# Gated-linear-attention level products cut to 64 by 64 on both halves of the array, gathered into one run a head

## The chip, the cores and the metric

The kernel runs on one core of one Trainium2 chip. Times are device microseconds of one execution. The kernel before took 2210.24 us as the median of 3 runs (2208.63 to 2212.44). Its profile is one further execution.

The engines are called as in the profile: PE is the matrix engine (PEld its weight loads), DVE the vector engine, ACT the scalar engine, POOL the general engine, SP the engine that issues most DMAs. A line number such as L873 is a line of the kernel before.

## What is computed

One layer of a hybrid decoder over 2048 tokens and 16 leading meta tokens, width 1024, everything in float32:

```
u      = RMSNorm(h);  proj = u @ w_in                 # one combined projection
y_ssd  = SSD branch   (16 heads of 64, 4 groups, state 128, chunk 128)
y_gla  = GLA branch   (4 heads, key width 128, value width 256)
out    = RMSNorm(h + (sum_b sigmoid(g_b) * (y_b @ w_branch[b])) @ w_out)
```

The change lies in the gated linear attention (GLA). For one head and one chunk of tokens it needs, for every pair t >= s,

```
gc   = cumsum(log_a)                                  # per key channel k
att[t, s] = sum_k q[t,k] * k[s,k] * exp(gc[t,k] - gc[s,k])
o    = att @ v  +  (q * exp(gc)) @ state
```

The factor exp(gc[t] - gc[s]) can't be split into one factor of t and one of s without overflow over a whole chunk, so the kernel works in levels, described below.

## The kernel before, in words

**Stages.** The 2048 tokens go in four blocks of 512. In the first part of the kernel (to about 1445 us of the profile) each block is projected and both branches are computed; in the second part come the merge gates, the branch products and the output product. The change touches the first part only.

**Levels.** `gla_scan` handles one head of one block: 512 tokens as four chunks of 128 (`NCH`). For each half in `LEVELS` = 64, 32, 16, 8, 4, 2, `level_in` (L845) takes the gates relative to the middle of every group of 2*half tokens (a DVE subtraction, L858), exponentiates both sides on ACT (L861, L862), and multiplies the first half of each group with the keys (L863) and the second half with the queries (two instructions of L865) into one tile `kq`. Chunks lie in pairs in it: the query half of one chunk takes the place that the key half of its neighbour leaves free, so that one 128 by 128 product serves two chunks. `level_out` (L869) then makes two such products a level (L873), each float32 product being two PE instructions, and puts the result into a tile `xa` of 128 by 2 by 128: with a copy on ACT for level 64 (L877), under a mask on DVE (`copy_predicated`, L880) for the others. Of a level below 64 only the 64 by 64 blocks on the diagonal are used, of level 64 only the two off it. The pairs at distance one and the diagonal come from sums over the key channel with a matrix of ones (L945); they are merged at L947 to L953 into `att`, which holds all four chunks. `split` turns `att` into a rounded part and a rest (`atp`), the odd chunks after a transposition (L960).

**Ticks.** `enter` walks through the pieces of projection of a block: a piece is some 24 products of 512 columns. After each piece `step` runs every begun generator up to its next `yield`; that is a tick. So PE sees: a piece, then what each scan has in this tick, then the next piece. A GLA scan begins every sixth piece. In a scan of the kernel before, the first tick has `level_in(64)`; the second `turn_keys` (a transposition of the keys, L894), levels 32 and 16 in and level 64 out; the third 8 and 4 in, 32 and 16 out; the fourth 2 in, 8 and 4 out, and the operands `pn`, `pd` of the sums; the fifth level 2 out, the sums and the merge; the sixth the transpositions and the first half of `advance`; the seventh and eighth the outputs (L981 and the products after it); the tenth the transposition of the output (L1000, drained by L1001 on DVE).

**Where scans meet.** In blocks 1 and 2 (counting from 0) the heads begin behind pieces 30, 36, 42 and 48 (the last is the first piece of the next block), so the fourth tick of one head is the tenth of the head before it. Piece 36 to 39 is `proj_v12`, which holds three banks of PSUM pool `pj` and one of `pt`. In the last block heads 2 and 3 begin inside `proj_v12` and `proj_v`, behind pieces 39 and 43, and there `step` goes through the scans from the youngest to the oldest.

**What sets the order.** The order on PE and SP is the one in which the program is written (`manual_schedule`). The order on DVE, ACT and POOL is chosen beforehand by a planner that simulates the program; `issue_after(x)` puts what a block of code issues on x's engine behind x. Each engine then runs its queue in that order and waits for its operands and for free buffers.

**Buffers.** SBUF tiles of one tag share `bufs` slots. Tag `sq` (2 KB a partition, 6 slots) serves `ex` and `kq` of the levels, `pd` and its split, `att`, and in `ssd_scan` the masked scores `scm` and four decay tiles `dm` a group. Tag `xd` (1 KB, 4 slots) holds `xdt` of `ssd_scan`; tag `c1` (1 KB, 8 slots) serves `xa`, `pn` and its split, the states, `xw` and `yo`. PSUM has three banks each in `pj` and `pt` and two in `pc`; a level's products lie in `pc`, as do the outputs of `advance`, L981 and the inner product of `ssd_scan`. That inner product (`inside`, L717) is already cut in two: 64 columns of weights, 64 moving columns, written to partitions 0 to 63 and 64 to 127 in turn, 32 products (64 instructions) in one run.

Of the kernel before, what the change touches and what calls it, by code (L numbers as in the profile page):

```python
# [8 lines left out]
F32 = mybir.dt.float32  # L9
# [3 lines left out]
AF = mybir.ActivationFunctionType  # L13
ALU = mybir.AluOpType

P = 128
# [3 lines left out]
BLK = 512  # L20
NCH = BLK // P
# [2 lines left out]
NH = 16  # L24
EPS = 1e-6
NWR = 3
NSQ = 6
NT4 = 5
NACT = 8
NC1 = 8  # L30
NAS = 6
LATE_G = 2
LEVELS = (64, 32, 16, 8, 4, 2)
# [10 lines left out]
def trunk_kernel(ctx: ExitStack, tc: tile.TileContext, xm, xmt, w_feat, w_tok, w_v3, w_zm, w_br, w_o,  # L44
                 cf32, cmsk, pvec, fnw, hvec, gw2, out):
    nc = tc.nc
# [5 lines left out]
    def mk(pool, shape, dt, tag, **kw):  # L52
        cnt[0] += 1
        return pool.tile(shape, dt, tag=tag, name=f"{tag}_{cnt[0]}", **kw)
# [72 lines left out]
    bpool, wk, sm, const = pool1("bpool", 1), pool1("wk", 2), pool1("sm", 4), pool1("const", 1)  # L127
# [4 lines left out]
    pc = ctx.enter_context(tc.tile_pool(name="pc", bufs=2, space=bass.MemoryType.PSUM))  # L132
# [4 lines left out]
    def bank(pool, tag):  # L137
        return mk(pool, [P, 512], F32, tag)
# [5 lines left out]
    tris = cst[:, 2:4, :]  # L144
# [126 lines left out]
    def split(h, lo, src):  # L271
        nc.scalar.activation(h, src, AF.Copy)
        nc.vector.tensor_tensor(lo, src, h.bitcast(F32), op=ALU.subtract)
# [117 lines left out]
    msk = const.tile([P, NMSK, P], U8, name="msk")  # L391
# [86 lines left out]
    def gates(o):  # L478
        m0, tt, chunks, g_all = o.m0, o.tt, o.chunks, o.g_all
        ast = (act_tile(F32R) if m0 else mk(wk, [P, BLK], F32R, "sq", bufs=NSQ))[:48, :tt]  # L480
        for a, n in ([(0, META), (m0, BLK)] if m0 else [(0, BLK)]):
# [135 lines left out]
            feats.append(f)  # L617
            yield

    cbs, evicted, convd = {}, [], []  # L620

    def behind():
        return tc.issue_after(evicted[-1].ins) if evicted else nullcontext()
# [6 lines left out]
    def ssd_scan(o, g):  # L630
# [7 lines left out]
        def hb(t, n):  # L638
            return t.unsqueeze(2).to_broadcast([n, 4, 64])

        if m0:
            ps = bank(pt, "pt")
# [20 lines left out]
                                tri.unsqueeze(1).to_broadcast([P, NCH, P]), op=ALU.mult)  # L663
        yt = mk(wk, [P, NCH, 256], F32, "tok4", bufs=NT4)
        ssq = mk(sm, [P, 4], F32, "ssq")
        held, intra = {}, {}

        def before(c):
            a = m0 + c * P
            ci = ci0 + c  # L670
            if c + 1 < NCH:
                fetch_cb(o, g, c + 1)
            cb = cbs.pop((g, c))
            ps = bank(pt, "pt")
            for j, f in enumerate((x0, x1, bf)):
                nc.tensor.transpose(ps[:, j * P:(j + 1) * P], f[:, a:a + P], ident)
            px = ps[:, :256].rearrange("p (h c) -> p h c", c=64)
            xdt = mk(wk, [P, 4, 64], F32, "xd", bufs=NCH)
            nc.vector.tensor_tensor(xdt, px, hb(tkd[:, ci, hs], P), op=ALU.mult)
            xw = mk(wk, [P, 4, 64], F32, "c1", bufs=NC1)  # L680
            nc.vector.tensor_tensor(xw, px, hb(wde[:, ci, hs], P), op=ALU.mult)
            nc.vector.tensor_tensor(yt[:, c].rearrange("p (h c) -> p h c", c=64), px,
                                    hb(d_skip[:, hs], P), op=ALU.mult)
            bt = mk(wk, [P, P], F32, "bt")
            nc.scalar.activation(bt, ps[:, 256:384], AF.Copy)
            dm = mk(wk, [P, 4, P], F32, "sq", bufs=NSQ)
            with behind() if o.b == 0 else nullcontext():
                for h in range(4):
                    nc.scalar.activation(dm[:, h], cb[:, h], AF.Relu, scale=-1.0,
                                         bias=tkc[:, ci, 4 * g + h:4 * g + h + 1])  # L690
                nc.scalar.activation(dm, dm, AF.Exp, scale=-1.0)
            convd[:] = [nc.vector.tensor_tensor(dm, dm, scm[:, c].unsqueeze(1).to_broadcast([P, 4, P]), op=ALU.mult)]
            held[c], intra[c] = (xw, bt), (xdt, dm)
# [53 lines left out]
        r = rstd_of(ssq, 4, 1.0 / 1024)  # L747
# [5 lines left out]
        for j in range(2):  # L753
            ps = bank(pt, "pt")
# [56 lines left out]
    def gla_scan(o, h, last=False):  # L811
# [27 lines left out]

        xa = mk(wk, [P, 2, P], F32, "c1", bufs=NC1)
        kqs = {}

        def level_in(half):  # L845
            nb = BLK // (2 * half)
            npc = P // (2 * half)

            def view(t):
                return t.rearrange("p (b two h) -> p b two h", two=2, h=half)  # L850

            def view5(t):
                return t.rearrange("p (r o b two h) -> p r o b two h", o=2, b=npc, two=2, h=half)

            ex = mk(wk, [P, BLK], F32, "sq", bufs=NSQ)
            kq = mk(wk, [P, BLK], F32, "sq", bufs=NSQ)
            ev = view(ex)
            nc.vector.tensor_tensor(  # L858
                ex.rearrange("p (b s) -> p b s", s=2 * half), gr.rearrange("p (b s) -> p b s", s=2 * half),
                view(gr)[:, :, 0, half - 1:half].to_broadcast([P, nb, 2 * half]), op=ALU.subtract)  # L860
            nc.scalar.activation(ev[:, :, 0], ev[:, :, 0], AF.Exp, scale=-ITEMP)  # L861
            nc.scalar.activation(ev[:, :, 1], ev[:, :, 1], AF.Exp, scale=ITEMP)  # L862
            nc.vector.tensor_tensor(view(kq)[:, :, 0], ev[:, :, 0], view(k)[:, :, 0], op=ALU.mult)  # L863
            for i in range(2):
                nc.vector.tensor_tensor(view5(kq)[:, :, 1 - i, :, 1], view5(ex)[:, :, i, :, 1],  # L865
                                        view5(q)[:, :, i, :, 1], op=ALU.mult)
            kqs[half] = kq

        def level_out(half):  # L869
            kq = kqs.pop(half)  # L870
            ps = bank(pc, "pc")
            for r in range(2):
                nc.tensor.matmul(ps[:, r * P:(r + 1) * P], kq[:, 2 * r * P:(2 * r + 1) * P],  # L873
                                 kq[:, (2 * r + 1) * P:(2 * r + 2) * P], start=True, stop=True)
            pv2 = ps[:, :256].rearrange("p (r t) -> p r t", t=P)
            if half == 64:
                nc.scalar.activation(xa, pv2, AF.Copy)  # L877
            else:
                mi = msk[:, LEVELS.index(half)].unsqueeze(1).to_broadcast([P, 2, P])
                nc.vector.copy_predicated(xa, mi, pv2)  # L880

        level_in(64)
        yield
        if m0:
            ps = bank(pt, "pt")
# [5 lines left out]
        def turn_keys():  # L891
            ps = bank(pt, "pt")
            for c in range(NCH):
                nc.tensor.transpose(ps[:, c * P:(c + 1) * P], kd[:, m0 + c * P:m0 + (c + 1) * P], ident)  # L894
            kdt.extend(beside_64("kdt") for _ in range(2))
            split(*[t.rearrange("p c t -> p (c t)") for t in kdt], ps)

        if not last:
            turn_keys()
        level_in(32)  # L900
        level_out(64)
        level_in(16)
        yield
        if m0:
            ps = bank(pt, "pt")
            nc.tensor.matmul(ps[:, :256], btm[:META], s_gla[:META, h], start=True, stop=True)
            nc.vector.tensor_copy(s_gla[:, h], ps[:, :256])
        level_out(32)
        level_in(8)
        level_out(16)  # L910
        level_in(4)
        yield
        level_out(8)
        level_in(2)
        level_out(4)


        def halves(t):
# [1 line left out]

        pn = mk(wk, [P, 2, P // 2, 2], F32, "c1", bufs=NC1)
        for i in range(2):
# [12 lines left out]
            split(*hl, src)  # L935
            parts.append((hl, n))
        yield
        if last:
            turn_keys()
        level_out(2)  # L940
        sums_ = []
        for hl, n in parts:
            ps = bank(pt, "pt")
            for i in range(2):
                nc.tensor.matmul(ps[:, :n], ones_r, hl[i], start=i == 0, stop=i == 1)  # L945
            sums_.append(ps)
        nc.vector.copy_predicated(xa, msk[:, len(LEVELS)].unsqueeze(1).to_broadcast([P, 2, P]),  # L947
                                  sums_[0][:, :256].rearrange("p (r t) -> p r t", t=P))
        att = mk(wk, [P, NCH, P], F32, "sq", bufs=NSQ)
        nc.vector.tensor_tensor(att.rearrange("p (r o) t -> p r o t", o=2),  # L950
                                xa.unsqueeze(2).to_broadcast([P, 2, 2, P]),
                                tris.unsqueeze(1).to_broadcast([P, 2, 2, P]), op=ALU.mult)
        nc.vector.copy_predicated(att, msk[:, 0].unsqueeze(1).to_broadcast([P, NCH, P]),  # L953
                                  sums_[1].rearrange("p (c t) -> p c t", t=P))
        atp = [beside_64("atp") for _ in range(2)]
        split(*[t[:, 0::2] for t in atp], att[:, 0::2])
        yield
        ps = bank(pt, "pt")
        for r in range(2):
# [30 lines left out]
        with tc.issue_after(summed[-1].ins) if o.b == nblk - 1 and h == GH - 1 and summed else nullcontext():  # L990
            r = rstd_of(ssq, 4, 1.0 / 256)
# [5 lines left out]
        for j in range(2):  # L997
            ps = bank(pt, "pt")
# [68 lines left out]
    for b in range(nblk):  # L1067
        o = new_block(b, next_u[b])
        last = b == nblk - 1
# [331 lines left out]
    for si, st in enumerate(stages):  # L1401
        for q in range(0 if si else 12, 28):
            p, j = PS[q // 4], q % 4
# [12 lines left out]
    for key, st in zip(late, (stages[0], stages[-4])):  # L1416
        i, end = begins[stages.index(st)] + 9, begins[stages.index(st) + 1] - 16
# [88 lines left out]
def _layout(inputs):  # L1506
# [36 lines left out]
    row, col = idx[:, None], idx[None, :]  # L1543
    cf32[:, 2] = col > row
    cf32[:, 3] = col < row
    cmsk = np.zeros((P, NMSK, P), f)
    cmsk[:, 0] = np.eye(P)
    for i, h in enumerate(LEVELS + (1,)):
        if i:
            cmsk[:, i] = (row // (2 * h) == col // (2 * h)) & (row // h != col // h)  # L1550

    def pcol(v):
        return v.reshape(-1, P).T
# [37 lines left out]
```

## Time and profile before

| | |
|---|---|
| median of 3 runs | 2210.24 us (2208.63 to 2212.44) |
| the profiled execution | 2209.51 us, of which the profile's span is 2207.7 us |
| first part, to 1445 us | PE busy 1419.2 of 1445 us |
| second part | PE busy 755.3 of 762 us |
| level products (L873) | 384 instructions, 24 a head and block, 16 of these |
| granted PE clock | 0.997 in the mean |

How to read it: busy time of PE counts a matrix product from its start to its modelled end, and neighbours overlap. What a product takes out of PE's time is therefore the step from one start to the next, not its duration. "Idle before" names what ended a wait of the engine just before an instruction. A wait of an engine that isn't the bound costs nothing by itself.

### The profile page before, as it was taken

How to read it: one execution, taken by the hardware profiler on the slowest of the kernel's cores; microseconds unless marked ns; L12 is line 12 of the kernel's file. 1: busy time of each engine (PE TensorE's matmuls, PEld its weight loads, DVE VectorE, ACT ScalarE, POOL GpSimd, SP SyncE). 2: the span in 40 equal slices, each digit the busy share in tenths (PEclk: the TensorE clock that was granted, in tenths of full speed). 3: DMA queues.
4: the chain of work that ended last, by engine and by line, in shares of the span. 5: the costliest groups of instructions: out<-in, count | busy, mean ns of one | idle time of the engine just before them, and what ended most of it. 6: DMA issues, size and time to landing. Idle time of an engine off the chain costs nothing.

```text
span 2207.7 us, 35845 instructions
## 1 busy us (share of the span) xinstructions
PE 2174.5 (98%) x12301; PEld 1867.9 (85%) x12301; DVE 1553.8 (70%) x2871; ACT 1188.5 (54%) x2767; POOL 693.8 (31%) x689
## 2 busy tenths in 40 slices
PE   7999999999999999999999999999999999999998
PEld 7999889888888988888988888878888888888887
DVE  5786675677577676658677666674789955789876
ACT  5666655466455456545465554464644545554544
POOL 5444433222222122221222100166233374324341
PEclk9999999999999999999999999999999999999999
DMA  9766775667778677778677664376768866787753
GB/s 316 254 228 235 255 271 211 218 217 244 257 253 265 210 227 230 249 257 274 208 223 238 215 216 161 124 265 214 246 221 297 304 223 216 240 286 255 255 187 121
DMA packets 313702, 518.00 MB, mean 235 GB/s; under 512 B 28080, under 2 KB 162480, under 8 KB 313520
## 3 DMA queue, kind: packets, MB, share of 16 engines
q1 hardware_dynamic: 247008, 419.89, 58.3%
q10 hardware_dynamic: 65872, 93.74, 11.6%
q8 instruction: 96, 1.57, 0.3%
q0 software_dynamic: 640, 2.10, 0.2%
q14 instruction: 86, 0.70, 0.1%
HBM read 368.42 MB, written 147.19 MB: 234 GB/s over the span
## 4 chain that ended last, share of the span: by engine, by line
PE 86%; DVE 4%; ACT 3%; DMA 3%; POOL 1%; issue 1%; SPq 1%; POOLq 0%; ACTq 0%; DVEq 0%
PE pj L223 19%; PE pj L225 19%; PE pj L224 19%; PE pt L225 4%; PE pt L224 4%; PE pt L223 4%; PE pc L223 2%; PE pc L224 2%; PE pc L225 2%; PE pc L873 2%; PE pc L717 1%; PE pc L701 1%; PE pc L981 1%; PE pc L700 1%; DVE acc L612 1%
## 5 line engine op out<-in xcount | busy, mean ns | idle before, releaser
L223 PE MATMUL pj<-ue,whl 128*128 128x512 f32 (+2 forms) x672 | 236.7, 352 | 2.3 <-ACT acc L608 2.2
L224 PE MATMUL pj<-ue,whl 128*128 128x512 f32 (+2 forms) x672 | 228.9, 341 | 0.0
L225 PE MATMUL pj<-ue,whl 128*128 128x512 f32 (+2 forms) x672 | 228.5, 340 | 0.0
L223 PE MATMUL pj<-uo,whl 128*128 128x512 f32 x512 | 206.0, 402 | 0.0
L225 PE MATMUL pj<-uo,whl 128*128 128x512 f32 x512 | 199.9, 390 | 0.0
L224 PE MATMUL pj<-uo,whl 128*128 128x512 f32 x512 | 199.5, 390 | 0.0
L223 PE MATMUL pj<-b,a 128*128 128x512 f32 (+1 forms) x484 | 187.4, 387 | 0.5 <-DVE io L1304 0.5
L224 PE MATMUL pj<-b,a 128*128 128x512 f32 (+1 forms) x484 | 187.4, 387 | 0.0
L225 PE MATMUL pj<-b,a 128*128 128x512 f32 (+1 forms) x484 | 187.4, 387 | 0.0
L612 DVE SCALAR_TENSOR_TENSOR acc<-cin,hcw,acc 128x512 f32<-128x512 f32 (+1 forms) x192 | 156.1, 813 | 29.2 <-ACT acc L608 27.5
L1157 POOL TENSOR_TENSOR as<-ar,ar 128x512 f32<-128x512 f32 x38 | 58.3, 1534 | 371.4 <-DMA ar<-in_w_br 124.7
L83 POOL TENSOR_TENSOR wr<-wr 128x256 f32<-128x256 f32 x80 | 69.7, 871 | 332.2 <-DMA wr<-y 142.0
L1186 DVE TENSOR_TENSOR a<-ar,a 128x512 fp32r<-128x512 f32 x160 | 132.1, 834 | 58.8 <-ACT a L1185 57.8
L223 PEld LDWEIGHTS pj<-ue,whl 128*128 128x128 f32 x672 | 127.2, 189 | 18.3 <-ACT acc L608 3.1
L186 POOL TENSOR_TENSOR whl<-wr,whl 128x512 fp32r<-128x512 f32 (+1 forms) x76 | 102.6, 1357 | 122.0 <-ACT whl L184 93.4
L225 PEld LDWEIGHTS pj<-ue,whl 128*128 128x128 f32 x672 | 127.1, 189 | 14.4
L224 PEld LDWEIGHTS pj<-ue,whl 128*128 128x128 f32 x672 | 127.7, 190 | 13.3
L1186 DVE TENSOR_TENSOR a<-as,a 128x512 fp32r<-128x512 f32 x120 | 104.8, 875 | 41.5 <-ACT a L1185 38.2
L1185 ACT ACTIVATE a<-ar 128x512 fp32r<-128x512 f32 x160 | 99.1, 626 | 58.6 <-PE pt L225 22.1
L1220 ACT ACTIVATE sn<-pj 128x512 f32<-128x512 f32 x118 | 70.2, 595 | 110.8 <-PE pj L225 71.0
L224 PE MATMUL pt<-b,a 128*128 128x512 f32 x320 | 124.5, 389 | 0.0
L225 PE MATMUL pt<-b,a 128*128 128x512 f32 x320 | 124.5, 389 | 0.0
(335 smaller groups left out, 6367.9 us busy)
## 6 DMA issues: line engine op xcount, KB each, us to landing
whl<-k_s SPq DMA_DIRECT2D x96, 512.0 KB, 4.1
whl<-k_g SPq DMA_DIRECT2D x96, 512.0 KB, 4.5
whl<-k_v SPq DMA_DIRECT2D x36, 512.0 KB, 3.8
wr<-in_w_feat SPq DMA_DIRECT2D x64, 256.0 KB, 4.1
k_s<-whl SPq DMA_DIRECT2D x32, 512.0 KB, 3.8
cb<-cumd SPq DMA_DIRECT2D x64, 256.0 KB, 4.7
y<-gg ACTq DMA_DIRECT2D x64, 256.0 KB, 4.2
k_g<-whl SPq DMA_DIRECT2D x32, 512.0 KB, 3.7
```

Of the source, the lines that this page charges most:

```text
L83: nc.gpsimd.tensor_tensor(o, x, y, op=ALU.subtract)
L186: nc.gpsimd.tensor_tensor(hl[:, 1], raw, hl[:, 0].bitcast(F32), op=ALU.subtract)
L223: nc.tensor.matmul(ps, sh, mh, start=first, stop=False, **kw)
L224: nc.tensor.matmul(ps, sh, ml, start=False, stop=False, **kw)
L225: nc.tensor.matmul(ps, sl, mh, start=False, stop=last, **kw)
L612: convd[:] = [nc.vector.scalar_tensor_tensor(acc, cin[:, k:k + tt], hcw[:, ti, k:k + 1], acc, op0=ALU.mult, op1=ALU.add)]
L700: nc.tensor.matmul(ps[:, :256], cf[:, a:a + P], s_ssd[:, g], start=True, stop=True)
L873: nc.tensor.matmul(ps[:, r * P:(r + 1) * P], kq[:, 2 * r * P:(2 * r + 1) * P], kq[:, (2 * r + 1) * P:(2 * r + 2) * P], start=True, stop=True)
L1157: nc.gpsimd.tensor_tensor(s1, a21, a22, op=ALU.add)
L1185: nc.scalar.activation(t[:, 0], src, AF.Copy)
L1186: latest[:] = [nc.vector.tensor_tensor(t[:, 1], src, t[:, 0].bitcast(F32), op=ALU.subtract)]
L1220: nc.scalar.activation(sn, self.ps[n, "a"], AF.Copy)
```

## The change

Six edits:

1. Each level product of 128 by 128 is replaced by two of 64 by 64, one on each half of the array's columns (`levels_out`): 4 products a level and 24 a head, for 12 before.
2. All six levels of a head are multiplied in one run, in the fourth tick, into two `pc` banks taken together: levels 64, 32, 16, 8 in the first, 4 and 2 in the second. The merge moves from the fifth tick to the fourth; the fifth then has only `turn_keys` of the very last head.
3. Operands come two levels a tick: 64 and 32, then 16 and 8, then 4 and 2 with `pn` and `pd`.
4. `xa` shrinks to 128 by 2 by 64. Level 64 is copied straight into `att` by two ACT instructions of 64 partitions, the places opposite are zeroed by two POOL memsets, level 32 is copied by ACT, and 16, 8, 4, 2 follow under the mask on DVE, 128 elements a partition. The pairs at distance one and the product with the triangle are done in two instructions of 64 partitions each. The masks are built for this layout.
5. The subtraction of the next head's level 64 is put behind the last instruction of the merge (`merged`).
6. Buffers: `sq` has 3 slots for 6; a new tag `kq` with 6 slots of 2 KB holds the six `kq` tiles, and in `ssd_scan` the `dm` tiles and two `xdt` tiles at a time (tag `xd` goes); `c1` has 6 slots for 8; `xa` has its own.

```diff
-NSQ = 6
+NSQ = 3
+NKQ = 6
-NC1 = 8
+NC1 = 6
...
-            xdt = mk(wk, [P, 4, 64], F32, "xd", bufs=NCH)
+            if c % 2 == 0:
+                pair[:] = [mk(wk, [P, 2, 4, 64], F32, "kq", bufs=NKQ)]
+            xdt = pair[0][:, c % 2]
...
-            dm = mk(wk, [P, 4, P], F32, "sq", bufs=NSQ)
+            dm = mk(wk, [P, 4, P], F32, "kq", bufs=NKQ)
...
-        xa = mk(wk, [P, 2, P], F32, "c1", bufs=NC1)
+        xa = mk(wk, [P, 2, 64], F32, "xa", bufs=1)
...
-            kq = mk(wk, [P, BLK], F32, "sq", bufs=NSQ)
+            kq = mk(wk, [P, BLK], F32, "kq", bufs=NKQ)
...
-        def level_out(half):
-            kq = kqs.pop(half)
-            ps = bank(pc, "pc")
-            for r in range(2):
-                nc.tensor.matmul(ps[:, r * P:(r + 1) * P], kq[:, 2 * r * P:(2 * r + 1) * P],
-                                 kq[:, (2 * r + 1) * P:(2 * r + 2) * P], start=True, stop=True)
-            pv2 = ps[:, :256].rearrange("p (r t) -> p r t", t=P)
-            if half == 64:
-                nc.scalar.activation(xa, pv2, AF.Copy)
-            else:
-                mi = msk[:, LEVELS.index(half)].unsqueeze(1).to_broadcast([P, 2, P])
-                nc.vector.copy_predicated(xa, mi, pv2)
-
-        level_in(64)
+        def levels_out(att):
+            ps = [bank(pc, "pc").rearrange("p (l r t) -> p l r t", r=2, t=64) for _ in range(2)]
+            pl = [ps[n // 4][:, n % 4] for n in range(len(LEVELS))]
+            for n, half in enumerate(LEVELS):
+                kq = kqs.pop(half)
+                for r in range(2):
+                    for i in range(2):
+                        j = 1 - i if half == 64 else i
+                        nc.tensor.matmul(pl[n][i * 64:i * 64 + 64, r],
+                                         kq[:, 2 * r * P + i * 64:2 * r * P + i * 64 + 64],
+                                         kq[:, (2 * r + 1) * P + j * 64:(2 * r + 1) * P + j * 64 + 64],
+                                         start=True, stop=True)
+            for i in range(2):
+                rows, off = slice(i * 64, i * 64 + 64), slice(64 - i * 64, P - i * 64)
+                nc.scalar.activation(att[rows, i::2, off], pl[0][rows], AF.Copy)
+                nc.gpsimd.memset(att[rows, 1 - i::2, off], 0.0)
+            nc.scalar.activation(xa, pl[1], AF.Copy)
+            for n in range(2, len(LEVELS)):
+                nc.vector.copy_predicated(xa, msk[:, n, :64].unsqueeze(1).to_broadcast([P, 2, 64]), pl[n])
+
+        with tc.issue_after(merged[-1].ins) if merged else nullcontext():
+            level_in(64)
+        level_in(32)
         yield
...
         if not last:
             turn_keys()
-        level_in(32)
-        level_out(64)
         level_in(16)
+        level_in(8)
         yield
...
-        level_out(32)
-        level_in(8)
-        level_out(16)
         level_in(4)
-        yield
-        level_out(8)
         level_in(2)
-        level_out(4)
...
         yield
-        if last:
-            turn_keys()
-        level_out(2)
+        att = mk(wk, [P, NCH, P], F32, "sq", bufs=NSQ)
+        levels_out(att)
         sums_ = []
...
+        near = sums_[0][:, :256].rearrange("p (r t) -> p r t", t=P)
+        for rows, on in quads:
+            nc.vector.copy_predicated(xa[rows], msk[rows, len(LEVELS), :64].unsqueeze(1).to_broadcast([64, 2, 64]),
+                                      near[rows, :, on])
+        for rows, on in quads:
+            nc.vector.tensor_tensor(att[rows, :, on].rearrange("p (r o) t -> p r o t", o=2),
+                                    xa[rows].unsqueeze(2).to_broadcast([64, 2, 2, 64]),
+                                    tris[rows, :, on].unsqueeze(1).to_broadcast([64, 2, 2, 64]), op=ALU.mult)
+        merged[:] = [nc.vector.copy_predicated(att, msk[:, 0].unsqueeze(1).to_broadcast([P, NCH, P]),
+                                               sums_[1].rearrange("p (c t) -> p c t", t=P))]
         atp = [beside_64("atp") for _ in range(2)]
         split(*[t[:, 0::2] for t in atp], att[:, 0::2])
+        yield
+        if last:
+            turn_keys()
         yield
```

More of the change, by code (lines that the diff above doesn't have):

```diff
@@ L618, in proj_conv @@
             yield
-    cbs, evicted, convd = {}, [], []
+    cbs, evicted, convd, merged = {}, [], [], []
     def behind():
@@ L665, in ssd_scan @@
         ssq = mk(sm, [P, 4], F32, "ssq")
-        held, intra = {}, {}
+        held, intra, pair = {}, {}, []
         def before(c):
@@ L867, in level_in @@
             kqs[half] = kq
-        def level_out(half):
-            kq = kqs.pop(half)
-            ps = bank(pc, "pc")
-            for r in range(2):
-                nc.tensor.matmul(ps[:, r * P:(r + 1) * P], kq[:, 2 * r * P:(2 * r + 1) * P],
-                                 kq[:, (2 * r + 1) * P:(2 * r + 2) * P], start=True, stop=True)
-            pv2 = ps[:, :256].rearrange("p (r t) -> p r t", t=P)
-            if half == 64:
-                nc.scalar.activation(xa, pv2, AF.Copy)
-            else:
-                mi = msk[:, LEVELS.index(half)].unsqueeze(1).to_broadcast([P, 2, P])
-                nc.vector.copy_predicated(xa, mi, pv2)
-        level_in(64)
+        quads = [(slice(i * 64, i * 64 + 64), slice(j * 64, j * 64 + 64)) for i, j in ((0, 0), (1, 1))]
+        def levels_out(att):
[20 more added lines that the diff above has]
+        level_in(32)
         yield
@@ L946, in gla_scan @@
             sums_.append(ps)
[L947 to L954, printed above, removed]
+        near = sums_[0][:, :256].rearrange("p (r t) -> p r t", t=P)
[8 more added lines that the diff above has]
+                                               sums_[1].rearrange("p (c t) -> p c t", t=P))]
         atp = [beside_64("atp") for _ in range(2)]
         split(*[t[:, 0::2] for t in atp], att[:, 0::2])
+        yield
+        if last:
+            turn_keys()
         yield
@@ L1549, in _layout @@
         if i:
-            cmsk[:, i] = (row // (2 * h) == col // (2 * h)) & (row // h != col // h)
+            near = (row % 64 // (2 * h) == col // (2 * h)) & (row % 64 // h != col // h)
+            cmsk[:, i] = near & (col < 64)
     def pcol(v):
```

## The prediction

> **What bounds the kernel now.** I read the page first (span, busy time, slices, chain), then the list of what PE waited for.
>
> ```profile
> span 2207.7 us, 35845 instructions
> PE 2174.5 (98%) x12301; PEld 1867.9 (85%) x12301; DVE 1553.8 (70%) x2871; ACT 1188.5 (54%) x2767; POOL 693.8 (31%) x689
> PE   7999999999999999999999999999999999999998
> PE 86%; DVE 4%; ACT 3%; DMA 3%; POOL 1%; issue 1%; SPq 1%; POOLq 0%; ACTq 0%; DVEq 0%
> ...
> PE pt L333 <- DMA cst<-in_cf: 10.3, 1, 10.3
> PE pj L223 <- ACT acc L608: 4.3, 4, 2.1
> PE pc L223 <- DVE c L969: 2.8, 3, 2.1
> ```
>
> PE is busy in every slice after the first, and 86% of the chain that ended last is PE. Its largest wait, 10.3 us, lies at the start of the kernel; the next two make 7.1 us. So PE is the bound all through the part that is changed: what is taken out of its queue comes off the time one for one, and what makes it wait is added one for one. The groups by line show what the levels cost, and what DVE has to do with them.
>
> ```profile
> L873 PE MATMUL pc<-sq 128*128 128x128 f32 x384 | 53.4, 276 | 0.0
> L717 PE MATMUL pc<-xd,sq 128*64 128x64 f32 x1024 | 33.4, 224 | 0.0
> L880 DVE COPY_PREDICATED c<-msk,pc 128x256 f32<-128x256 uint8 x80 | 35.6, 446 | 43.1 <-PE pc L873 40.6
> L863 DVE TENSOR_TENSOR sq<-sq,act 128x256 f32<-128x256 f32 x96 | 46.5, 485 | 39.9 <-ACT sq L861 16.0 <-PE pc L873 13.0 <-PE pc L717 5.7
> ```
>
> The reader is to see two things. L873 never waits, while DVE stands 40.6 us in front of L880 and 13.0 us in front of L863 until PE has come to a level product: DVE is ahead of PE, not behind. And L717 is the shape that the change wants, 64 columns of weights and 64 moving columns on alternating halves, 1024 of them in this trace.
>
> **The products.** Busy time overlaps, so I price both shapes by their steps in PE's timeline (block 1).
>
> ```profile
> 635.71 0.39 PE L225 MATMUL pj<-uo,whl 128*128 128x512 f32 x1
> 635.94 1.05 PE L873 MATMUL pc<-sq 128*128 128x128 f32 x8
> 636.75 0.48 PE L223 MATMUL pj<-uo,whl 128*128 128x512 f32 x1
> 637.06 0.40 PE L224 MATMUL pj<-uo,whl 128*128 128x512 f32 x1
> ...
> 608.04 0.39 PE L225 MATMUL pj<-uo,whl 128*128 128x512 f32 x1
> 608.36 2.08 PE L717 MATMUL pc<-xd,sq 128*64 128x64 f32 x64
> 610.38 0.50 PE L223 MATMUL pj<-uo,whl 128*128 128x512 f32 x1
> 610.71 0.39 PE L224 MATMUL pj<-uo,whl 128*128 128x512 f32 x1
> ```
>
> A product of 512 columns steps 0.23 us (635.71 to 635.94). Eight level instructions reach from 635.94 to 637.06 less that step: 0.89 us, 111 ns each. The 64 of L717 reach from 608.36 to 610.71 less 0.23: 2.12 us, 33.1 ns each; going in costs 0.32 - 0.23 = 0.09 us more than a plain step. A head has 24 instructions now (384 over 16 heads), 24 x 0.111 = 2.67 us. After: 24 products of two instructions, 48 x 0.0331 + 0.09 = 1.68 us. That is 0.99 us a head and **15.8 us** for 16.
>
> Weighed against it: the Trainium skill, TensorEngine Tiling (Array Packing), under Key Properties, says that a change of tiling mode drains the array; by the 0.09 us above the trace agrees, and it is in the sum (1.4 us of the 16 heads).
>
> **DVE, ACT and POOL.**
>
> ```profile
> L950 DVE TENSOR_TENSOR sq<-c,cst 128x512 f32<-128x512 f32 x16 | 11.5, 721 | 0.4
> L877 ACT ACTIVATE c<-pc 128x256 f32<-128x256 f32 x16 | 5.9, 371 | 0.3 <-PE pc L873 0.3
> ```
>
> A head loses five L880 (446 ns), one more mask of that width and L950: 3.4 us of DVE. It gets six masks of 128 elements (two of them on half the partitions) and two half-height products of 256: between nothing and the old widths' prices, 6 x 446 + 2 x 721 ns = 4.1 us; by L863, the row of that width, a product is 485 ns, and the sum 3.6 at most. So DVE is about even. On ACT one copy (L877, 371 ns) becomes three shorter ones, at most 0.7 us more; on POOL come two memsets. I put all this at nothing: DVE is idle 30% of the span, ACT 46%, POOL 69%, and nothing on PE needs the merge for two more ticks, since the transpositions stay in the sixth. Without that cover it would be up to 1.4 us a head (0.7 on each of DVE and ACT). The change issues no DMA; SP's queue has only the pieces' loads in the old order.
>
> **Operands in time.** All six levels must be ready at the fourth tick. I compare the old place of the products there with DVE's last preparation (levels, then the two splits that the sums need).
>
> ```profile
> 633.52 0.69 DVE L273 TENSOR_TENSOR sq<-sq,sq 128x512 fp32r<-128x512 f32 x1 [0.22 <-ACT sq L272]
> ...
> 1384.49 1.05 PE L873 MATMUL pc<-sq 128*128 128x128 f32 x8
> 1386.15 0.49 DVE L865 TENSOR_TENSOR sq<-sq,act 128x128 f32<-128x128 f32 x2
> ...
> 1370.76 0.42 DVE L863 TENSOR_TENSOR sq<-sq,act 128x256 f32<-128x256 f32 x1 [2.34 <-PE pc L873]
> ```
>
> In block 1's first head the last split ends at 634.21, 1.7 us before PE's fourth tick at 635.94; it is needed only behind the run, 1.7 us later again. Only the third head of the last block is behind: its last level ends at 1386.64, 2.1 us after 1384.49. But DVE had lost 2.34 us at 1370.76 waiting for a level product to free a slot, and the six `kq` slots, all emptied by one run, take that wait away. I put it at 0, between 0 and 2.1. The `merged` edge only holds back one subtraction that DVE has time for. With `sq` at three, three exponents are in flight; `pd`, its split and `att` take turns there as `ex` ends.
>
> **Banks.** Here the change adds waits, on PE, and every later product is queued behind them. The sums' two `pt` banks are now wanted in the tick in which the head before takes two for its output (L1000) and, at piece 39 of blocks 1 to 3, `proj_v12` still holds the third.
>
> ```profile
> 642.64 0.48 PE L945 MATMUL pt<-c,ones_r 128*128 128x256 f32 x2
> 642.96 0.63 PE L945 MATMUL pt<-sq,ones_r 128*128 128x512 f32 x2
> ...
> 678.17 1.04 PE L1000 MATMUL pt<-cst,ot 128*128 128x128 f32 x8
> 679.04 1.06 PE L873 MATMUL pc<-sq 128*128 128x128 f32 x8
> ...
> 681.06 0.74 DVE L1001 SCALAR_TENSOR_TENSOR gg<-pt,hgw,gg 128x512 f32<-128x512 f32 x1
> 682.05 0.74 DVE L1001 SCALAR_TENSOR_TENSOR gg<-pt,hgw,gg 128x512 f32<-128x512 f32 x1
> 683.91 0.42 DVE L273 TENSOR_TENSOR tok<-pt,tok 128x256 fp32r<-128x256 f32 x1
> ...
> 721.23 0.75 DVE L1001 SCALAR_TENSOR_TENSOR gg<-pt,hgw,gg 128x512 f32<-128x512 f32 x1 [1.94 <-PE pt L1000]
> ...
> 1021.62 1.06 PE L873 MATMUL pc<-sq 128*128 128x128 f32 x8
> 1023.36 0.75 DVE L1001 SCALAR_TENSOR_TENSOR gg<-pt,hgw,gg 128x512 f32<-128x512 f32 x1
> 1024.35 0.75 DVE L1001 SCALAR_TENSOR_TENSOR gg<-pt,hgw,gg 128x512 f32<-128x512 f32 x1
> ...
> 1362.38 1.05 PE L873 MATMUL pc<-sq 128*128 128x128 f32 x8
> 1365.88 0.41 DVE L273 TENSOR_TENSOR tok<-pt,tok 128x256 fp32r<-128x256 f32 x1
> ```
>
> Block 1: the run would end at 679.04 + 1.68 = 680.72; the first bank comes free at 681.80 (1.1 us late), the first sum takes 0.32 (642.64 to 642.96), and the second bank comes at 682.79, 0.7 late: 1.8 us. Block 2 in the same way: 1023.30 against 1024.11 and 1024.43 against 1025.10, 1.5 us. In block 3 the young head goes first: run and sums end at 1362.38 + 1.68 + 0.32 + 0.46 (two steps of 0.23) = 1364.84, then L1000 wants `proj_v12`'s bank, free at 1366.29, 1.5 us late, and a second one out of the merge; I take 2. Elsewhere DVE stands ready for L1000, as at 721.23 (piece 45 of block 1, after a wait of 1.94 us), and nothing is added.
>
> ```profile
> 1385.15 0.44 DVE L880 COPY_PREDICATED c<-msk,pc 128x256 f32<-128x256 uint8 x1
> 1385.65 0.70 PE L981 MATMUL pc<-s_gla,act 128*128 128x256 f32 x2
> ```
>
> The run also takes both `pc` banks. Twice in the last block an older head wants one right behind it (L981). Before, L981 came 1.16 us after 1384.49, where eight instructions take 0.89, so 0.27 late, released by one L880. After, the first bank waits for three ACT copies and two masks, at most 3 x 0.37 + 2 x 0.45 = 2 us, of which two levels and the sums cover 1.3: 0.7 each, 1.4 together. The Trainium skill, same page, PSUM Bottleneck, warns that tiling speeds up the products and not the emptying of PSUM; that is this wait, by its rule at most those 2 us twice. Sum of waits: 1.8 + 1.5 + 2 + 1.4 = **6.7 us**, between 0 (the planner drains these banks first) and 14 (the rival of worse banks, below).
>
> **The sum.** -15.8 + 6.7 = -9.1 us: 2200.4 for the profiled execution of 2209.5 (span 2207.7 and 1.8 around it). The median shown is 0.7 above that execution, so 2201.
>
> **Rivals.**
> - *No bank waits.* DVE's order is planned anew, with the sums in the fourth tick in view; L1001 may then go ahead of the `tok` splits. For it: elsewhere DVE already stands ready for L1000. Against: at piece 39 it didn't. It gives -15.8: 2194.
> - *Banks handed out worse.* The planner gives the first sum `proj_v12`'s bank, free at 683.91 + 0.42 = 684.33 and not at 681.80: 2.5 us more at three places, 7.6 in all: -1.5, 2209. The last block's operands late by their 2.1 belong here too.
> - *Slower: DVE no longer ahead.* A level goes DVE, ACT, DVE through an `ex` slot, of which there are three for six of `sq`; if these, with the edge behind the merge, hold back the levels, PE stands before the run at every head. It decides from 9.1 / 16 = 0.57 us a head on. At 2 us a head it is +32 - 9: 2233. For it: the wait of 16.0 us of L863 on ACT. Against: the 53.6 us that DVE itself waited for PE.
> - *The cut doesn't pay.* If an instruction cost as much with half the columns, 48 at 111 ns would take 5.3 us, +2.7 a head, +43 and the 6.7 of waits: 2260. It decides from 45 ns on ((2.67 - 0.09 - 6.7 / 16) / 48). L717 with 33 ns in the same queue speaks against it. The Trainium skill, TensorE: Matmul & The Clock Gate, under "Wait — 56ns, not 53.3ns?", gives a floor of about 62 ns a product where the sequencer decodes in microcode, by which a run would be 48 x 62 ns = 3.0 us (an estimate from that page) and the time 2223; L717's steps of 33 ns show that this floor isn't in force here.
>
> **How the numbers follow.** A measurement of this kernel tells apart about 0.2%, 4.4 us: faster is below 2205.8, slower above 2214.7. Chances: forecast 0.50 (own range 2198 to 2205), no waits 0.26, worse banks 0.14, DVE late 0.08, no pay 0.02. The first two are faster; of the third I take most as the same: faster 0.77, same 0.13, slower 0.10. The range runs from 2193, the rival without waits and 1 us of scatter, to 2210, the rival of worse banks: some 0.85 of the chance.
>
> **What would show it.** Right: the run's 48 instructions step by 33 ns, about 1.6 us a run, 16 runs; no 128 by 128 level products; PE waits on L1001 or on a `tok` split at piece 39 of blocks 1 to 3, 1 to 2 us each; L981 waits on a mask twice; DVE's 40.6 us before L880 shrink to one wait a head. Wrong: steps of 45 ns or more; waits of PE for L865 or the exponents before the run; a saving in the second part, which isn't touched.

## The result, and the profile after

| | before | after |
|---|---|---|
| median | 2210.47 us (2208.63 to 2212.76, 5 runs) | 2225.65 us (2219.51 to 2232.11, 5 runs) |
| ratio after / before | | 1.0064, 95% interval 1.0041 to 1.0088 |
| profiled execution, its span | 2209.51, 2207.7 us | 2232.11, 2230.3 us |

The change made the kernel 0.6% slower; 2201 had been forecast. The profiled execution is the slowest of the five: its mean granted clock is 0.993, that of the other four 0.995 to 0.996. Ratios, here and below, leave out two disturbed executions of the experiments, one of 3111 us (the kernel before) and one of 7691 us (states). The page of the changed kernel, its first lines:

```profile
span 2230.3 us, 36756 instructions
PE 2169.2 (97%) x12685; PEld 1851.4 (83%) x12685; DVE 1537.9 (69%) x2887; ACT 1193.3 (54%) x2799; POOL 697.1 (31%) x721
```

PE is busy 5.3 us less, DVE 15.9 us less, and yet the span is 22.6 us longer: PE waits more. **The products** did what they should. The timeline of PE after, the first head of block 1, and the second, at piece 39:

```profile
636.03 0.39 PE L226 MATMUL pj<-uo,whl 128*128 128x512 f32 x1
636.35 1.62 PE L882 MATMUL pc<-kq 128*64 128x64 f32 x48
637.90 0.50 PE L951 MATMUL pt<-c,ones_r 128*128 128x256 f32 x2
638.24 0.63 PE L951 MATMUL pt<-sq,ones_r 128*128 128x512 f32 x2
...
682.77 1.62 PE L882 MATMUL pc<-kq 128*64 128x64 f32 x48
685.88 0.51 PE L951 MATMUL pt<-c,ones_r 128*128 128x256 f32 x2 [1.50 <-DVE gg L1012]
686.87 0.73 PE L951 MATMUL pt<-sq,ones_r 128*128 128x512 f32 x2 [0.48 <-DVE gg L1012]
```

From the last projection product to the second sum is 638.24 - 636.03 = 2.21 us. In the kernel before the same stretch, with four old products in it, took 0.91 us (642.05 to 642.96, quoted below); less these four at 111 ns, 0.47 us of it is no level product. A run therefore costs 2.21 - 0.47 = 1.74 us, where I had 1.68; against 2.67 us before, 0.93 us a head, 14.9 us in all. At piece 39 of block 1 the bank waits stand as forecast (1.50 + 0.48 us; 1.8 had been worked out).

**Where the time went.** From the list of what PE waited for, after (us in total, times, longest):

```profile
PE pc L224 <- DVE c L980: 7.9, 5, 2.4
PE pj L224 <- ACT act L773: 5.5, 2, 3.1
...
PE pc L992 <- DVE c L980: 3.9, 2, 2.0
PE pt L499 <- ACT sq L490: 3.4, 3, 1.1
PE pc L703 <- DVE s_ssd L707: 3.3, 3, 1.1
PE pt L951 <- DVE gg L1012: 2.5, 3, 1.5
...
PE pt L1011 <- DVE gg L1012: 1.3, 1, 1.3
PE pj L224 <- ACT act L769: 0.9, 1, 0.9
PE pc L992 <- DVE xa L892: 0.7, 2, 0.4
```

All rows of this view together are 53.2 us after and 25.2 us before: +28.0. Forecast had been the rows of L1012 and L892, some 4.5 us of it. The largest that grew are 11.8 us for L980, the states, which empty the bank of `advance` (L969 before, with 2.8 us), and 6.4 us for the evictions of the next head's keys and queries (L773, L769), which before has no row for. The rows of L490 and L707 lie outside the GLA heads; they come up again with states. No row has PE waiting for a level's operand.

Most of the longer pauses also have a stretch at half clock beside them. The busy times by window of the changed kernel, and below of the kernel before (columns: window, its length, busy time of PE, PEld, DVE, ACT, POOL; then granted PE clock, DMA share, GB/s):

```profile
105.00:111.80 6.80, 6.14 (x29) 6.15 (x30) 6.75 (x13) 5.08 (x15) 2.03 (x3) 0.50 0.50 154
303.00:309.80 6.80, 4.54 (x20) 4.25 (x21) 6.72 (x16) 4.80 (x15) 2.50 (x4) 0.50 0.94 299
658.00:661.40 3.40, 3.40 (x11) 2.63 (x9) 3.40 (x9) 2.47 (x8) 0.00 (x0) 0.51 0.44 92
1009.50:1012.90 3.40, 3.40 (x10) 2.62 (x9) 3.37 (x9) 3.29 (x10) 0.00 (x0) 0.50 0.33 115
1060.70:1067.50 6.80, 5.54 (x16) 4.67 (x17) 6.36 (x18) 5.34 (x16) 0.40 (x2) 0.50 0.11 41
```
```profile
107.30:110.70 3.40, 3.40 (x18) 3.40 (x18) 3.40 (x8) 3.19 (x10) 1.69 (x2) 0.50 0.07 25
233.60:237.00 3.40, 3.40 (x10) 2.67 (x9) 1.71 (x5) 1.72 (x5) 3.17 (x4) 0.50 0.66 235
305.30:308.70 3.40, 3.40 (x17) 3.40 (x17) 3.30 (x8) 3.40 (x13) 1.85 (x1) 0.50 0.81 257
```

27.2 us at half clock lose up to 13.6, the 10.2 us before up to 5.1: 8.5 us more. The account of the profiled executions: -14.9 (products) + 28.0 (waits) + 8.5 (clock) = +21.6, of +22.6 measured. The medians differ by 15.2 us only: most of the 6.5 us by which this execution is above its median is clock (an estimate: 0.0025 less in the mean, of 2225 us, is 5.6 us).

**Why the states are late.** The timeline of DVE and PE after, second head of block 2 (some lines left out):

```profile
1046.52 0.73 DVE L961 COPY_PREDICATED sq<-msk,pt 128x512 f32<-128x512 uint8 x1
1047.15 1.28 DVE L861 TENSOR_TENSOR sq<-g_all 128x512 f32<-128x512 f32 x2
...
1050.01 0.28 PE L226 MATMUL pc<-tok,kdt 128*128 128x256 f32 x1
...
1052.85 1.03 DVE L868 TENSOR_TENSOR kq<-sq,act 128x128 f32<-128x128 f32 x2
...
1058.03 0.47 DVE L980 SCALAR_TENSOR_TENSOR c<-s_gla,egl,pc 128x256 f32<-128x256 f32 x1
1058.55 0.70 PE L992 MATMUL pc<-c,act 128*128 128x256 f32 x2 [2.02 <-DVE c L980]
...
1061.03 0.48 DVE L868 TENSOR_TENSOR kq<-sq,act 128x128 f32<-128x128 f32 x2
1061.44 0.47 DVE L980 SCALAR_TENSOR_TENSOR c<-c,egl,pc 128x256 f32<-128x256 f32 x1
...
1061.96 0.58 PE L224 MATMUL pc<-tok,kdt 128*128 128x256 f32 x1 [2.35 <-DVE c L980]
```

PE has filled the bank of `advance` at 1050.29. DVE has no gap in the whole stretch, but spends most of it on L861, L866 and L868, the levels of the *next* head. PE multiplies these in the tenth tick of this head, and wants the states in its seventh; the states start 7.7 and 11.2 us after PE has finished. By then PE has done a whole piece, and stands: first for the state, then for the bank. The levels aren't late, as in my slower rival, but too early. The planner put them there when it ordered DVE's queue; my reading, which no run tests by itself, is that with six slots for `kq` alone nothing holds the six levels back. Between merge and second state of the first head DVE does 12 level instructions in the trace of before, and 22 in that of after.

### The profile page after: what moved, and what is told of

The parts are those of the page before. It is cut to its first block, busy times and chain, and to the rows that moved or that the text cites. A ratio compares the mean times of both kernels' runs of the same rounds, so it can differ in the third digit from the quotient of the medians.

```text
span 2230.3 us, 36756 instructions
## 1 busy us (share of the span) xinstructions
PE 2169.2 (97%) x12685; PEld 1851.4 (83%) x12685; DVE 1537.9 (69%) x2887; ACT 1193.3 (54%) x2799; POOL 697.1 (31%) x721
## 4 chain that ended last, share of the span: by engine, by line
PE 43%; DVE 4%; DMA 3%; issue 2%; ACT 1%; POOL 1%; SPq 0%; ACTq 0%; POOLq 0%; DVEq 0%
PE pj L224 9%; PE pj L226 9%; PE pj L225 9%; PE pt L226 3%; PE pt L225 3%; PE pt L224 3%; PE pc L224 2%; PE pc L226 2%; PE pc L225 2%; DMA br<-out_t 1%; DVE b L1153 1%; DMA br<-br_t 1%; DVE a L1197 1%; DMA io<-g 1%; DMA br<-in_w_o 0%
## 5 line engine op out<-in xcount | busy, mean ns | idle before, releaser
L613 DVE SCALAR_TENSOR_TENSOR acc<-cin,hcw,acc 128x512 f32<-128x512 f32 (+1 forms) x192 | 155.9, 812 | 35.1 <-ACT acc L609 33.7
L225 PEld LDWEIGHTS pj<-ue,whl 128*128 128x128 f32 x672 | 128.0, 190 | 13.6
L224 PE MATMUL pj<-whl,ue 128*128 128x256 f32 (+2 forms) x376 | 119.4, 317 | 9.2 <-ACT act L773 3.1
L1153 DVE TENSOR_TENSOR b<-br,b 128x512 fp32r<-128x512 f32 x124 | 107.7, 888 | 24.9 <-ACT b L1152 24.5
L226 PE MATMUL pt<-b,a 128*128 128x512 f32 x320 | 124.5, 389 | 0.0
```

Of the source, the lines that this page charges most:

```text
L224: nc.tensor.matmul(ps, sh, mh, start=first, stop=False, **kw)
L225: nc.tensor.matmul(ps, sh, ml, start=False, stop=False, **kw)
L226: nc.tensor.matmul(ps, sl, mh, start=False, stop=last, **kw)
L613: convd[:] = [nc.vector.scalar_tensor_tensor(acc, cin[:, k:k + tt], hcw[:, ti, k:k + 1], acc, op0=ALU.mult, op1=ALU.add)]
L1153: nc.vector.tensor_tensor(t[:, 1], raw, t[:, 0].bitcast(F32), op=ALU.subtract)
```

## The experiments

Ratios are to the kernel before in the same comparison. "Lag" is, for a head, the time from the end of the last product of its first `advance` to the start of the second state on DVE; in the lists of waits the columns are total, times, longest.

**1. Which part of the change costs?** Four kernels: the cut products alone, at their old four places a head and in the old buffers (shape); the changed kernel with the run in the fifth tick and the levels in the old ones (fifth); without edge 5 (noedge); with the memsets on DVE (memdve).

```diff
 shape, against before:
...
+                for i in range(2):
+                    j = 1 - i if half == 64 else i
+                    nc.tensor.matmul(ps[i * 64:i * 64 + 64, r * 64:r * 64 + 64],
+                                     kq[:, 2 * r * P + i * 64:2 * r * P + i * 64 + 64], ...
...
 noedge, against after:
-        with tc.issue_after(merged[-1].ins) if merged else nullcontext():
-            level_in(64)
+        level_in(64)
 memdve, against after:
-                nc.gpsimd.memset(att[rows, 1 - i::2, off], 0.0)
+                nc.vector.memset(att[rows, 1 - i::2, off], 0.0)
```

> The kernel before with the 64 by 64 products alone: the old ticks, one level or two at a time, the old buffers (sq 6, xd 4, c1 8); level 32 copied by ACT, the masks and the merge in the new layout, but level 64 multiplied with the triangle on DVE and no memset on POOL. Theory Q (the products pay, and the loss comes from queues and buffers): 24 products a head cost 1.6 us for 2.7, PE's waits stay near 25 us, time 2193 to 2198. Rival C (products on half the array let the granted clock drop): half-clock windows beyond those of before without longer waits ahead of them, time 2205 or more. Rival P (the shape doesn't pay): 2208 to 2212.

> The changed kernel (one run, new buffers, edge, memsets) with the operands and the run in the old ticks: 64, then 32 and 16, 8 and 4, 2 with the sums' operands, run and merge in the fifth. If the loss comes from two levels a tick and the run a tick earlier: 2195 to 2203, PE's waits under 32 us. If it comes from the buffers (three slots of sq) or from the one run: 2215 to 2230, waits on the states (L980) and on the q and k evictions stay.

> The changed kernel without the edge that puts the next head's level 64 behind the merge. If the edge packs the next head's levels into a burst that the evictions wait behind: under 2212. If not: 2218 to 2230, as the changed kernel.

> The changed kernel with the two memsets a head on DVE and not on POOL. POOL stood 88 us in front of these memsets, up to 15 us at a time. If what is queued behind them on POOL (the powers of the norms, the state's decay, the sums) holds PE: 2205 to 2213 and the waits on s_ssd, ot and the states shrink. If POOL's standing costs nothing: 2218 to 2230.

| | median us | ratio, 95% interval |
|---|---|---|
| shape | 2223.4 | 1.0062 (1.0047 to 1.0077) |
| fifth | 2233.54 | 1.0116 (1.0098 to 1.0133) |
| noedge | 2220.24 | 1.0054 (1.0033 to 1.0074) |
| memdve | 2230.43 | 1.0097 (1.0075 to 1.012) |

None of these parts, taken back, cures it, and shape alone is as slow as the whole. Two reasons. First the products: the timelines of PE before and in shape, at the last group of a head.

```profile
642.05 0.39 PE L225 MATMUL pj<-uo,whl 128*128 128x512 f32 x1
642.28 0.60 PE L873 MATMUL pc<-sq 128*128 128x128 f32 x4
```
```profile
640.48 0.39 PE L225 MATMUL pj<-uo,whl 128*128 128x512 f32 x1
640.79 0.45 PE L876 MATMUL pc<-sq 128*64 128x64 f32 x8
641.17 0.50 PE L950 MATMUL pt<-c,ones_r 128*128 128x256 f32 x2
641.51 0.63 PE L950 MATMUL pt<-sq,ones_r 128*128 128x512 f32 x2
```

Eight instructions of the new shape take 641.51 - 640.48 - 0.47 = 0.56 us, four of the old 0.44. With the 1.74 us of a run of 48 that gives (1.74 - 0.56) / 40 = 29.5 ns an instruction and 0.32 us for going in and out. In small groups the switch eats the gain; in one run it is paid once. Second, PE's waits: 37.1 us in shape for 25.2. The clock is not a third reason: shape's trace has two windows at half clock inside the kernel, that of before three. The largest new ones of shape, noedge and fifth, in that order:

```profile
PE pt L971 <- DVE sq L964: 5.3, 4, 2.6
...
PE pt L971 <- ACT gg L802: 2.7, 1, 2.7
```
```profile
PE pt L970 <- DVE sq L960: 15.2, 5, 5.0
```
```profile
PE pt L971 <- DVE sq L964: 18.1, 10, 6.1
```

In all three the largest is for the end of the merge (L964, L960), and in shape's and noedge's queue the next head's levels are ahead of it. After has the edge there, and so the levels lie ahead of the next thing that isn't tied, the states. That is a theory of **queue order**: DVE has time enough (69% busy), but does first what isn't urgent. Taking the memsets off POOL doesn't help (memdve). The rival is **slots**: three exponent slots for six levels; ACT stood up to 2.8 us with the split of `pd`, for such a slot, ahead of an eviction that PE wanted.

**2. Order, slots, or bad luck?** states moves the edge behind the second state of the first `advance` (which now returns that instruction), for two levels; shapeedge adds the edge behind the merge to shape; shared9 pools the slots; null leaves the kernel before as it is, but for one tiny instruction a head.

```diff
 states, against after:
-        merged[:] = [nc.vector.copy_predicated(att, ...)]
+        nc.vector.copy_predicated(att, ...)
...
-        advance(0)
+        merged[:] = [advance(0)]
...
         with tc.issue_after(merged[-1].ins) if merged else nullcontext():
             level_in(64)
-        level_in(32)
+            level_in(32)
 shared9, against after (all tiles of tag "kq" take tag "sq"):
-NSQ = 3
+NSQ = 9
 null, against before:
+        nc.vector.tensor_copy(gl[:, :NCH], gl[:, :NCH])
```

> The changed kernel, with the first two levels of the next head put on DVE's queue behind the states of the head before (the two instructions that empty the bank of its first advance, L980) in place of behind its merge. Queue-order theory: in the changed kernel DVE's queue holds 9 to 12 level products and 4 to 6 subtractions between merge and states, and PE stood 7.9 + 3.9 us for L980; these waits go, with the half-speed clock behind two of them (about 6 us): 2232 - 12 - 6 = 2214 for the profiled execution, and a median of 2205 to 2217. Rival, DVE has not the time: the levels now come too late for the run in the fourth tick, PE waits in front of it, and the time stays at 2222 or more.

> The kernel before with the 64 by 64 products at their old places (as in shape) and one edge more: the first level of the next head goes on DVE's queue behind the merge of the head before. Queue-order theory: in shape DVE's queue had two to four level products and subtractions of the next head ahead of the last instruction of the merge, and PE stood 8 us in front of the transpositions of att; these go, and the time is 2210 to 2216. Rival, the products in five small groups a head save too little (6 us) and their switches cost the rest: 2220 or more.

> The changed kernel with one tag of nine slots in place of three for the exponents and six for the products. Slot theory: DVE and ACT lost their time waiting for one of three exponent slots (the split of pd stood 2.6 to 2.8 us in front of an eviction); with nine in common the time falls by 5 us or more, to 2220 or less. Queue-order theory: the states still lie behind seven to ten level products on DVE's queue, PE waits for them as before, and the time stays at 2221 to 2232.

> The kernel before with one copy of four elements a partition more on DVE a head and block (a copy of a tile onto itself): no work worth naming, but the planner orders all queues anew. If the order of the kernel before is a lucky one and any new plan costs some us by chance, the time rises by 4 us or more, to 2212 to 2222. If plans differ little as long as buffers and ticks stay, it is within 2207 to 2212.

| | median us | ratio, 95% interval | longest lag of a head, us |
|---|---|---|---|
| after | 2225.65 | 1.0064 (1.0041 to 1.0088) | 11.5 |
| states | 2206.1 | 0.998 (0.9967 to 0.9993) | 4.6 |
| shapeedge | 2210.84 | 1.0005 (0.9992 to 1.0017) | 6.6 |
| shared9 | 2208.53 | 0.9994 (0.9985 to 1.0004) | 8.9 |
| null | 2211.2 | 1.0002 (0.9988 to 1.0015) | 8.3 |

In the kernel before the longest lag is 8.6 us. In after the six long ones (7.2 to 11.5) are those of the first and second head of blocks 0 to 2. The same place as above in the timeline of states:

```profile
1027.26 0.28 PE L226 MATMUL pc<-tok,kdt 128*128 128x256 f32 x1
...
1030.28 0.47 DVE L980 SCALAR_TENSOR_TENSOR c<-s_gla,egl,pc 128x256 f32<-128x256 f32 x1
...
1031.60 0.47 DVE L980 SCALAR_TENSOR_TENSOR c<-c,egl,pc 128x256 f32<-128x256 f32 x1
1032.00 1.89 DVE L861 TENSOR_TENSOR sq<-g_all 128x512 f32<-128x512 f32 x3
```

The states come first, the levels behind them, and PE doesn't stand. Of its waits in states, and of those in shared9:

```profile
PE pt L951 <- DVE gg L1013: 3.7, 6, 1.0
...
PE pt L1012 <- DVE gg L1013: 1.3, 1, 1.3
...
PE pc L993 <- DVE xa L892: 0.7, 2, 0.4
...
PE pc L224 <- DVE c L980: 0.5, 1, 0.5
```
```profile
PE pc L224 <- DVE c L980: 3.7, 3, 1.6
```

With the edge moved the loss is gone, and no row shows a level coming late: order is shown, and the rival of missing time falls. What is left in states are the banks that I had forecast, 3.7 + 1.3 + 0.7 = 5.7 us (6.7 forecast), and two rows that I hadn't: 3.7 us for L490, and 3.3 us for L707, where before has 1.9 us for L685 at the same product. L490 writes `ast`, a tile of the gates that in blocks 1 to 3 takes a slot of tag `sq` as well; its row stands in every list of a kernel with three such slots (3.4 to 4.3 us), and in none of the four with nine in common. The row of L707 stands in three of these four (3.1 to 4.1 us), so the slots don't settle it; what brings it stays open. All rows of states are 35.7 us, 10.5 more than before; with -14.9 for the products that makes -4.4 us, and the ratio says the same (-4.4, between -7.3 and -1.5). The profiled execution of states, 2201.75 us, is the fastest of its ten.

shapeedge says the same from the other side: the edge brings the sum of PE's waits from 37.1 us in shape to 27.3. In null one new plan cost nothing. But shared9 contradicts me: I had expected 2221 or more. Its queue still has 21 level instructions between merge and second state of the first head, yet the lag is shorter and L980 costs 4.7 us (3.7 and 1.0) for 11.8. PE only stands when the lag passes the piece in between: for the first head of block 0, 1.6 us at a lag of 8.9, and 1.9 + 2.3 us at 11.5. One wait that the common slots took away is ACT's in front of the split of `pd`, for an exponent slot (10.5 us in after, ended by L868; no such row in shared9); whether that alone shortened the lag isn't settled.

**3. One cure or two, and can the banks be had too?** both joins states and shared9; outlate is states with every head's output transposed one tick later, out of the way of the run; three is all of it.

```diff
 outlate, against states:
-        if o.b == nblk - 1 and h == GH - 1:
-            yield
+        yield
         for j in range(2):
             ps = bank(pt, "pt")
```

> The edge behind the states (states) and the nine common slots (shared9) together. In states 17 us of the loss went, in shared9 as much. If both cure the same thing, the waits for L980 and what they trigger, the two together give no more than one: 2203 to 2209. If slots and queue order are two separate losses, the second comes on top of the first: 2188 to 2198.

> states, with the transposition of every head's output one tick later (the eleventh, the fifth of the next head, in which nothing is done now), so that it no longer wants pt banks in the tick of the run and the sums. In states PE still stood 3.7 us for L1013 before the sums and 1.3 us between the output's transpositions, which is the bank wait that I had forecast. Bank theory: these go, 2206 - 5 = 2199 to 2203. Rival: the outputs now drain behind the merge on DVE, the gates' tiles come free a tick later, and the waits only change their place: 2204 to 2212.

> Edge behind the states, nine common slots and the later output together. If the three are separate: 2185 to 2197. If the slots add nothing to the edge: the time of outlate within 3 us.

both took 2202.09 us, 0.9964 (0.9952 to 0.9976); outlate 2224.28, 1.0059 (1.0046 to 1.0071); three 2221.59, 1.0044 (1.0027 to 1.006). both lies 0.9 us below what I had expected if the two cure the same loss, and far from the 2188 to 2198 of two losses: edge and slots cure one and the same, for the second adds some 4 us in the medians to the first, whose own gain over after is some 19. The later output failed: of outlate's waits the largest new one is

```profile
PE pt L677 <- DVE gg L1012: 9.2, 3, 3.6
```

The last head's output now holds its two `pt` banks when the next block's SSD scans want one for their first transposition, and DVE's queue has convolutions (L613) and the products of the decay tiles (L695) ahead of L1012. The bank wait wasn't removed but sent to a place where DVE is slower.

**4. The rest.** outmid is both, with the later output for heads 0 to 2 of blocks 0 to 2 only (and, as in the kernel before, for the last head of all); oldedge is the kernel before with the edge behind the states and nothing else.

```diff
 outmid, against both:
-        if o.b == nblk - 1 and h == GH - 1:
+        if (h == GH - 1) == (o.b == nblk - 1):
             yield
 oldedge, against before:
-        advance(0)
+        merged[:] = [advance(0)]
...
-        level_in(64)
+        with tc.issue_after(merged[-1].ins) if merged else nullcontext():
+            level_in(64)
```

> both, with the output's transposition one tick later only where the next head's run shares its tick and no new scan begins behind it (heads 0 to 2 of blocks 0 to 2, and the last head of all as before). Bank theory: the 3.2 us that PE stood for L1013 before the sums go, and nothing waits in their place, since the places where outlate lost (first transpositions of the next block's SSD scans, the last block) keep the old tick: 2202 - 3 = 2196 to 2201. Rival: the later drain costs the gates' tiles elsewhere: 2202 to 2210.

> The kernel before, its products and ticks untouched, with the edge alone: the next head's first level goes behind the states. If the gain of states over the kernel before were the edge's alone, this one would be as fast, 2202 to 2207. If the products make it, this one stays near the kernel before, whose PE stood only 2.8 us for these states: 2206 to 2211, or later where the levels then come late for their products.

outmid took 2199.85 us, 0.9963 (0.995 to 0.9976); oldedge 2209.87, 1.0006 (0.9998 to 1.0014). The edge is worth nothing where the levels aren't in the way, so what states, both and outmid win over the kernel before isn't the edge's; that it is the products' follows from their price, no run shows it apart. In outmid the wait of the sums for L1013 is gone from the list, and a new one stands in block 0, ending at 333.32 us:

```profile
PE pt L1012 <- DVE xa L955: 2.2, 1, 2.2
```

By its ratio it is no better than both, though its median is the lowest of all. Three versions beat the kernel before with an interval below 1: states by 0.2%, both and outmid by 0.4%.

## Why the prediction was wrong

- **The bound** (PE, and every wait of PE added one for one): right, and it was the whole result; more exactly a wait can cost more than itself, because of the clock.
- **The products** (1.68 us a run, 15.8 us saved): right in kind, 1.74 and 14.9. The split was off: I took 33.1 ns an instruction and 0.09 us for going in, so that the price of going out was spread over the instructions; it is 29.5 ns and 0.32 us. For the run of L717 from which I worked both give the same (0.09 + 2.12 and 64 x 0.0295 + 0.32, 2.21 us each), but not for groups of eight (0.35 against 0.56).
- **DVE, ACT and POOL at nothing**: here the prediction failed. That DVE would get no more work was right (15.9 us less). But I asked what DVE has to do and not in which order; "nothing on PE needs the merge for two more ticks" covers the merge only, and the states behind it have a deadline as well. L980 costs 11.8 us where it was 2.8, the evictions on ACT 6.4 where there was no row; states, which changes the order alone, brings them to 1.0 us and to nothing. Four of the five half-clock windows, 20.4 us, stand at these pauses.
- **Operands in time** (0): the number held, no operand was late. The reason I gave may be what did the harm: that six `kq` slots "take that wait away". I now read that wait of DVE for slots as a brake, which before kept part of the next head's levels behind the states (12 instructions ahead of the second state, 22 after). That is argued; no run changes the slots of `kq` alone. With `sq` at three I looked at the heads only and not at the gates, whose row (L490) is 3.4 us.
- **The edge** ("only holds back one subtraction that DVE has time for"): taken as a cost, at nothing. Without it the merge would have been late (15.2 us in noedge); with it the states are. It protected one instruction too few.
- **Banks** (6.7 us): L1012 and L892 made 4.5 us in after and 5.7 in states.
- **The rivals**: the slower one named DVE and the extra waits, with the wrong sign: levels held back, PE standing before the run. That its time, 2233, came nearest is luck: in after PE never stands before the run, and the long lags are those of six heads of sixteen.
- With the order alone put right, states gains 4.4 us by its ratio, of 9.1 forecast: 0.9 less from the products, and waits of 10.5 us where I had 6.7. both gains 8 us (0.0036 x 2210), but with other slots, and its list of waits sums to 35.7 us as well; where its 3.6 us more come from stays open.

## What to carry to other kernels

Where an engine's queue is ordered beforehand, an engine with idle time can still be the one that is late: for each instruction for which the bound engine waits, ask what the planner may now place ahead of it, and tie what isn't urgent behind it. A shortage of buffers may be what keeps early work back, so when tiles get slots of their own, check whether an edge has to take that place. A narrow shape of product pays in long runs: compare the fixed price of going in and out with what a group saves.

## What the runs showed of the hardware

- The granted clock can halve at pauses of PE far shorter than I had thought worth a term. In after each of the five windows at 0.50 begins within 2 us of the end of a pause or in it: 2.87 us ending at 105.66, 1.93 and 2.26 us ending at 301.85 and 305.69, 2.35 us at 656.67, 3.14 us at 1009.13, 2.02 and 2.35 us ending at 1058.55 and 1061.96. The windows are 3.4 or 6.8 us long. The Trainium skill, TensorE: Matmul & The Clock Gate, under "What's actually happening", has the halved clock after at least one idle window of about 3.4 us; none of these pauses was that long.
- A pause of that length needn't halve it: 2.40 us ending at 233.15 in after, 2.86 us at 105.14 in states and 2.96 us at 231.03 in shapeedge have a clock of 1.00 around them, while 2.87 us at 107.75 in shared9, the same wait as that of states, has a window at 0.50 behind it. Executions of one kernel differ in it too: 0.993 to 0.996 in the mean for the five of after, 0.995 to 0.999 for nine of states.
- Going into the 64-column shape and out again costs some 0.32 us a run. It is worked out from a group of 8 instructions (0.56 us) and the run of 48 (1.74 us), and the 64 of L717 agree (2.21 us).
